# A gated hybrid layer in fp32 on one core: half of the first gate becomes seven block products, MLA's heads follow one another sooner

## The chip, the cores and the metric

The kernel runs on one core of one Trainium2 chip. The core has five engines that run beside each other, each with a queue of its own that it works off in order: PE (TensorE: matmuls and transposes; its weight loads, PEld, overlap them), DVE (VectorE), ACT (ScalarE), POOL (GpSimd) and SP (SyncE, which here only issues DMAs). The metric is the device time of one execution in microseconds, as a median of several.

## What is computed

One layer of a decoder on 512 tokens with 2048 features, in float32, batch 1. Cut to what matters here:

```python
xn = rmsnorm(h, g_mix)
(q_a, k_c, ..., c_q, c_kv, k_r, gate_a, gate_b) = split(xn @ w_in)     # gate_a, gate_b: 2048 columns each
o_a = nsa_attention(...)                    # 16 heads
o_b = mla_attention(c_q, c_kv, k_r, ...)    # 16 heads
mixed = sigmoid(gate_a) * (o_a @ w_o_nsa) + sigmoid(gate_b) * (o_b @ w_o_mla)
h = h + mixed @ w_out
h = h + memory_cross_attention(rmsnorm(h), rmsnorm(mem), ...)   # 256 memory tokens, 4 heads of 128
h = h + square(relu(rmsnorm(h) @ w_ff1)) @ w_ff2
return rmsnorm(h, g_final)
```

The two gates are plain products of the normalised input, 512 x 2048 by 2048 x 2048 each. A sigmoid is made as (1 + tanh(half)) / 2.

## The kernel before

**A product in three matmuls.** Every operand is split into a high and a low part in PE's fp32r format: ACT casts the high part (L444, L447, L1534, L1616), DVE subtracts it to get the low one (L445, L448, L1539, L1621). A product is hi x hi + hi x lo + lo x hi, three matmuls (L437 to L439; in the block products L1765 to L1767).

**Two ways to make a large product.** *Plain chunk* (`chunk`, L546): 512 output columns, all 16 k tiles, four row tiles of 128 tokens; the weights come as a stream of units of 512 KB through `Stream`, loaded by SP into two raw buffers and split a few units ahead. *Block products* (`Mlp` and its kin): two by two blocks in rows and in the contraction, with sums of blocks in place of some products, so that seven products do the work of eight. For weights, the sums are made by the DMA itself, which adds what it reads to what lies there (`accum_op`, L1529); for x, DVE adds blocks (L1589 to L1595). `Gates` (L1954) makes the second gate so: 2 column groups of 1024, seven products each, `NP` = 14.

**Main work and side work.** Python writes each engine's instructions in one fixed order. `Side` (L348) holds attention as a queue of steps, each a few instructions for PE, DVE and ACT: an item of MLA (one head) has 5 steps of scores and 6 of values of the head before, 11 in all; NSA has two items per head. After each k tile of the main work, `side.run(rate)` writes `rate` steps, and one step of the *post*, which prepares what the last chunk left in the four row buffers R: rotary embedding (`rope`, L513, four instructions on POOL per row tile) and the turning of the heads to features (`heads_T`, L530: four transposes on PE, one for each row tile, then a split). A post that isn't through by the last k of the next chunk is written out there without main work between (`end_post`); `ft` doesn't do so. If `heads_T` finds no free slot of the 40 in SBUF, it waits for later steps to free one. An attention group of four heads yields empty steps until its four q and four k heads are turned (`mla_attend`, L1208).

**MLA's stage** (`mla`, L1213). `gate(c)` is a plain chunk of the first gate with Tanh at the end (L1152) and a store of each row tile to `d_g` by a DMA that POOL issues (L1153). `mla_q(q)` makes four heads' q (4 k tiles of 384 columns; post: four ropes, then four heads turned), `mla_kv(q)` their k and v (2 k tiles of 512 columns; post: four heads turned; POOL copies k's rotary part, L1188). The order before:

```
gate 0, q 0, kv 0, [attend 0], q 1, gate 1, kv 1, [attend 1], q 2, gate 2, kv 2, [attend 2],
q 3, gate 3 (feeds), kv 3, [attend 3], [flush]
```

with 4.4 steps per k tile up to kv 0 and 2.6 after it. While gate 3 runs, `fed` gives back the x tiles as they fall out of use and starts `mem_load` (L1266): it loads the memory tokens, and with each call splits one k tile of 128 x 256 (ACT, DVE) and adds its squares (ACT squares, L510; POOL adds, L511). Ten tiles are done in gate 3, six are left for the next stage.

**The memory and second gate's stage** (`mix`, L1237). `mem_k` (L1290) makes the k heads of the memory attention by `ft` (L578): one head is 16 k tiles of three matmuls with 256 columns, and a step of the post comes at every odd k. In head 0, each k also calls `mem_load`. Beside it x is loaded again for the second gate (`x_in`, L1970, SP) and scaled by its gain (`x_gain`, L1977: eight instructions on POOL, L1986, per half of 1024 features and 256 tokens). `mem_v` makes the values, with the first loads and splits of the second gate (`loads`, `ahead`). Then `Gates.run` (L2008): of a group's seven products, every odd half unit splits a weight unit and an x block; all weight loads are issued by POOL (`ONE`). `Mixed` and `Out` follow, with the first gate read back from `d_g`.

`pairs` are five larger buffers: three hold the split c_q and c_kv, two hold v of two attention groups; `mla_kv` takes one and, if none is free, writes side steps until one is.

## Time and profile before

| what | us |
|---|---|
| median of 3 runs | 2788.45 (2785.52 to 2789.39) |
| the profiled execution | 2789.09 |
| its span, first to last instruction | 2787.3 |
| Tanh of the first gate (L1152), first to last start | 605.6 to 861.0 |
| `mem_k`'s first matmul | 867.07 |
| second gate's first product to last Tanh (L2006) | 941 to 1092.2 |

The profile is one execution. Spans are in microseconds from its first instruction, and L437 is line 437 of the kernel. "Idle before" names how long an engine stood still before an instruction and what released it. Matmuls are pipelined: one of 512 columns has a printed length of 0.39 us, but the next starts sooner than that, so prices are read from the distance of starts. The mean granted clock of PE is 0.999.

### The profile page before, as it was taken

What the parts mean: (1) busy time and instruction counts of PE and PEld (TensorE: products, weight loads), DVE (VectorE), ACT (ScalarE), POOL (GpSimd) and SP (SyncE); (2) the same over time, 40 slices, a digit from 0 to 9 for tenths busy, and PEclk for the clock granted to TensorE, in tenths of its full rate; (3) what the DMA queues carried; (4) which work ended last, traced back from release to release, by engine and by line L of the source; (5) the groups of instructions that cost most, each with busy time, mean ns of one, the idle gap of its engine ahead of it and who ended that gap; (6) DMA issues with size and microseconds to landing.
All of it is one profiled execution on the core that took longest, in us unless ns stands there. A gap on an engine that the chain in (4) does not pass through costs nothing.

```text
span 2787.3 us, 37036 instructions
## 1 busy us (share of the span) xinstructions
PE 2765.3 (99%) x13428; PEld 2325.0 (83%) x13428; DVE 2034.2 (73%) x3217; ACT 1592.3 (57%) x2670; POOL 530.9 (19%) x796
## 2 busy tenths in 40 slices
PE   9999999999999999999999999999999999999998
PEld 8888889988888888888888888888888788888887
DVE  6347776766557886878866877777777788888888
ACT  5345556655557675556555766666666444444445
POOL 4021011011116232222200112111211121111111
PEclk9999999999999999999999999999999999999999
DMA  5331112222235798989814899888889998888986
GB/s 180 99 90 62 59 59 67 69 73 80 92 109 177 188 235 202 223 225 255 214 46 135 197 224 219 203 206 218 196 220 254 247 216 220 215 218 220 240 236 156
DMA packets 153383, 476.89 MB, mean 171 GB/s; under 512 B 15728, under 2 KB 40432, under 8 KB 153200
## 3 DMA queue, kind: packets, MB, share of 16 engines
q0 software_dynamic: 63616, 230.72, 39.8%
q1 hardware_dynamic: 71744, 226.25, 23.4%
q10 hardware_dynamic: 17840, 17.57, 1.9%
q8 instruction: 105, 1.72, 0.2%
q14 instruction: 78, 0.64, 0.1%
HBM read 443.01 MB, written 31.46 MB: 170 GB/s over the span
## 4 chain that ended last, share of the span: by engine, by line
PE 92%; DVE 3%; DMA 2%; ACT 2%; issue 1%; POOL 0%; DVEq 0%; ACTq 0%; POOLq 0%
PE mm L1767 10%; PE mm L1766 10%; PE mm L1765 10%; PE mm L437 9%; PE mm L439 8%; PE mm L438 8%; PE st L1767 7%; PE st L1765 7%; PE st L1766 7%; PE st L675 2%; PE o L1765 1%; PE o L1766 1%; PE o L1767 1%; PE st L438 1%; PE st L439 1%
## 5 line engine op out<-in xcount | busy, mean ns | idle before, releaser
L1765 PE MATMUL mm<-s,s 128*128 128x512 f32 x1392 | 545.4, 392 | 0.0
L1767 PE MATMUL mm<-s,s 128*128 128x512 f32 x1392 | 542.4, 390 | 1.1 <-DVE s L1621 1.0
L1766 PE MATMUL mm<-s,s 128*128 128x512 f32 x1392 | 541.8, 389 | 0.0
L1534 ACT CAST s<-d 128x1024 fp32r<-128x1024 f32 x272 | 282.3, 1050 | 245.7 <-DMA d<-wts 224.7
L437 PE MATMUL mm<-s,s 128*128 128x512 f32 (+5 forms) x1012 | 400.5, 396 | 0.0
L1539 DVE TENSOR_TENSOR s<-d,s 128x1024 fp32r<-128x1024 f32 x272 | 329.5, 1220 | 94.2 <-ACT s L1534 93.6
L1539 DVE TENSOR_TENSOR s<-s,s 128x1024 fp32r<-128x1024 f32 x252 | 304.9, 1221 | 105.4 <-ACT s L1534 103.3
L439 PE MATMUL mm<-s,s 128*128 128x512 f32 (+5 forms) x1012 | 381.6, 377 | 0.0
L438 PE MATMUL mm<-s,s 128*128 128x512 f32 (+5 forms) x1012 | 381.1, 377 | 0.0
L1534 ACT CAST s<-s 128x1024 fp32r<-128x1024 f32 x252 | 260.2, 1050 | 182.3 <-DMA s<-wts 161.5
L1765 PE MATMUL st<-s,s 128*128 128x512 f32 x920 | 360.6, 392 | 0.0
L1767 PE MATMUL st<-s,s 128*128 128x512 f32 x920 | 358.3, 389 | 0.0
L1766 PE MATMUL st<-s,s 128*128 128x512 f32 x920 | 358.1, 389 | 0.0
L1767 PEld LDWEIGHTS mm<-s,s 128*128 128x128 f32 x1392 | 261.3, 188 | 56.9 <-DVE s L1621 2.4
L1766 PEld LDWEIGHTS mm<-s,s 128*128 128x128 f32 x1392 | 261.4, 188 | 53.3
L1765 PEld LDWEIGHTS mm<-s,s 128*128 128x128 f32 x1392 | 261.4, 188 | 53.2 <-ACT s L1616 0.3
L1529 POOL DMA_DIRECT2D d<-wts x169 | 149.4, 885 | 813.1 <-DVE s L1539 662.3
L445 DVE TENSOR_TENSOR s<-s,s 128x512 fp32r<-128x512 f32 (+4 forms) x301 | 207.7, 700 | 94.9 <-ACT s L444 93.5
L444 ACT CAST s<-st 128x512 fp32r<-128x512 f32 (+4 forms) x249 | 112.3, 460 | 186.7 <-PE st L675 118.1
L439 PEld LDWEIGHTS mm<-s,s 128*128 128x128 f32 x1012 | 190.0, 188 | 32.6
L444 ACT CAST s<-s 128x512 fp32r<-128x512 f32 (+4 forms) x301 | 177.1, 603 | 59.6 <-PE mm L439 30.4
L437 PEld LDWEIGHTS mm<-s,s 128*128 128x128 f32 x1012 | 191.1, 189 | 20.9
(415 smaller groups left out, 4846.7 us busy)
## 6 DMA issues: line engine op xcount, KB each, us to landing
s<-wts SPq DMA_DIRECT2D x203, 512.0 KB, 3.7
d<-wts POOLq DMA_DIRECT2D x203, 512.0 KB, 8.2
s<-wts POOLq DMA_DIRECT2D x156, 512.0 KB, 8.2
d<-wts SPq DMA_DIRECT2D x69, 512.0 KB, 7.7
PP<-wts POOLq DMA_DIRECT2D x65, 512.0 KB, 8.5
d_u<-s ACTq DMA_DIRECT2D x64, 256.0 KB, 5.0
PP<-wts SPq DMA_DIRECT2D x27, 512.0 KB, 6.5
s<-d_u SPq DMA_DIRECT2D x16, 512.0 KB, 11.8
```

The source lines that it names most:

```text
L437: t.matmul(ps, a.hr, b.hr, start=first, stop=False)
L438: t.matmul(ps, a.hr, b.lr, start=False, stop=False)
L439: t.matmul(ps, a.lr, b.hr, start=False, stop=last)
L444: nc.scalar.copy(o.hr, src)
L445: nc.vector.tensor_sub(o.lr, src, o.hi)
L675: nc.tensor.transpose(ps[:rows, i * 128:i * 128 + 128], p, self.ident)
L1529: self.nc.gpsimd.dma_start(t, src, accum_op=OP.add)
L1534: self.nc.scalar.copy(t.hr, self.raw[i])
L1539: self.nc.vector.tensor_sub(t.lr, r, t.hi)
L1765: m(ps, a.hr, b.hr, start=first, stop=False, skip_group_check=True)
L1766: m(ps, a.hr, b.lr, start=False, stop=False, skip_group_check=True)
L1767: m(ps, a.lr, b.hr, start=False, stop=last, skip_group_check=True)
```

## The change

Columns 1024 to 2047 of the first gate are no longer two plain chunks. They become a third column group of `Gates`, ahead of the two of the second gate: seven more block products, whose result is stored to `d_g` by SP. The loads of the first of all these products are issued by SP and no longer by POOL. MLA's order becomes:

```
gate 0, kv 0, q 0, [attend 0], kv 1, q 1, [attend 1], gate 1 (feeds), kv 2, q 2, [attend 2],
mem_k heads 0 and 1, kv 3, q 3, [attend 3], [flush], mem_k heads 2 and 3, mem_v, second gate
```

with 4.4 steps per k tile up to q 1 and in group 3, and 4.0 in gate 1 and group 2; 1.25 (0.8 before) per two k of `mem_k`, 2.3 (1.8 before) per k tile of `mem_v`. To make room for two groups' heads, the last four x tiles are given back before kv 1; in gate 1 they are loaded again (k = 3) and split again (k = 7 to 10). `mem_load` begins at k = 6 of gate 1 and does eight tiles there (k = 8 to 15), so eight are left for head 0 of `mem_k`. `x_in` and `x_gain` move: the first block's `x_gain` stands ahead of `mem_k` head 2, and the block (1, 1) moves to `mem_v`.

```diff
-T = dict(pace=0.75, r0=4.0, r1=4.4, rm=2.6, rf=4.4, rk=0.8, rv=1.8, rg=1.4)
+T = dict(pace=0.75, r0=4.0, r1=4.4, rm=4.0, rf=4.4, rk=1.25, rv=2.3, rg=1.4)
...
-    for c in range(4):
+    for c in range(2):
         for i in range(8):
             u["ga", c, i] = pack(w[2 * i:2 * i + 2, :, O_GA + 512 * c:O_GA + 512 * c + 512])
-    gb = np.ascontiguousarray(w[:, :, O_GB:O_GB + D]).reshape(2, 4, 2, 128, 2, 2, 512)
-    for c in range(2):
+    gb = np.ascontiguousarray(w[:, :, O_GA + D // 2:O_GB + D]).reshape(2, 4, 2, 128, 3, 2, 512)
+    for c in range(3):
...
     def mla(self, rate):
+        last = range(KT - 4, KT)
         def fed(k):
             if k:
                 self.put(self.X[k - 1])
             if k == 3:
+                self.xagain = [self.slots.get() for _ in range(2)]
+                self.xraw = {i: self.xagain[i % 2][:, 512 * (i // 2 % 2):512 * (i // 2 % 2) + 512] for i in last}
+                for i in last:
+                    self.nc.sync.dma_start(self.xraw[i], self.a["xT"][i])
+            if 6 < k < 11:
+                i = k + KT - 11
+                self.X[i] = self.slot_hl()
+                self.split(self.X[i], self.xraw[i], self.gains[:, G_MIX + i:G_MIX + i + 1])
+            if k == 11:
+                self.put(*self.xagain)
+            if k == 6:
                 self.ml = self.mem_load()
-            if k == 3 or k > 5:
+            if k == 6 or k > 7:
                 next(self.ml)
         self.gate(0, T["rf"])
+        ks, vs = self.mla_kv(0, T["rf"])
         qs = self.mla_q(0, T["rf"])
-        ks, vs = self.mla_kv(0, T["rf"])
-        for q in range(3):
+        self.side.add(self.mla_attend(0, qs, ks, vs))
+        self.put(*(self.X[i] for i in last))
+        ks, vs = self.mla_kv(1, T["rf"])
+        qs = self.mla_q(1, T["rf"])
+        self.side.add(self.mla_attend(1, qs, ks, vs))
+        self.gate(1, rate, fed)
+        self.put(self.X[-1])
+        for q in range(2, 4):
+            r = T["rf"] if q == 3 else rate
+            ks, vs = self.mla_kv(q, r)
+            qs = self.mla_q(q, r)
             self.side.add(self.mla_attend(q, qs, ks, vs))
-            qs = self.mla_q(q + 1, rate)
-            self.gate(1 + q, rate, fed if q == 2 else None)
             if q == 2:
-                self.put(self.X[-1])
-            ks, vs = self.mla_kv(q + 1, rate)
-        self.side.add(self.mla_attend(3, qs, ks, vs))
+                g = Gates(self)
+                self.mem_k(T["rk"], range(2), g)
         self.side.add(self.flush())
...
     def mix(self, g):
...
-        self.mem_k(T["rk"], g)
+        self.mem_k(T["rk"], range(2, 4), g)
...
     def mem_k(self, rate, hs, g):
...
-        for h in range(4):
-            if h < 3:
-                g.x_in(*((0, 0), (1, 0), (1, 1))[h])
-            if h:
-                g.x_gain(*((0, 0), (1, 0), (1, 1))[h - 1])
+        for h in hs:
+            if 0 < h < 3:
+                g.x_in(h - 1, 0)
+            if h > 1:
+                g.x_gain(h - 2, 0)
             ps = self.ft("mk", h, self.MX, rate, n=256, on_k=(on0, on1, None, None)[h])
...
     def mem_v(self, rate, g):
...
+            if u == 0:
+                g.x_in(1, 1)
+            if u == 1:
+                g.x_gain(1, 1)
...
+            self.put(self.mslots[u])
...
 # Mlp.load
-            (self.nc.gpsimd if self.ONE else self.nc.sync).dma_start(t, src)
+            (self.nc.gpsimd if self.one(p) else self.nc.sync).dma_start(t, src)
...
 class Gates(Mlp):
-    CH = 2
+    CH = 3
...
+    def one(self, p):
+        return p
...
     def use(self, p, ps):
...
         c, n = divmod(p, 7)
+        c -= 1
...
             nc.scalar.activation(o, ps[t] if n == 6 else o, AF.Tanh, scale=k.rxh[:, r:r + 1])
+            if c < 0:
+                nc.sync.dma_start(k.d_g[r, :, 1024 + 512 * b:1536 + 512 * b], o)
+                if n > 4:
+                    k.put(C.pop((r, c)))
...
             if n == 0:
-                X = [k.new_st() if p else k.new_mm() for _ in range(2)]
+                X = [k.new_st(), k.new_o() if p > 7 else k.new_st()] if p else [k.new_mm() for _ in range(2)]
```

More of the change, by code (lines that the diff above doesn't have):

```diff
@@ L1218, in fed, with mix @@
             if k == 3:
+                self.xagain = [self.slots.get() for _ in range(2)]
[9 more added lines that the diff above has]
+            if k == 6:
                 self.ml = self.mem_load()
-            if k == 3 or k > 5:
+            if k == 6 or k > 7:
                 next(self.ml)
         self.gate(0, T["rf"])
+        ks, vs = self.mla_kv(0, T["rf"])
         qs = self.mla_q(0, T["rf"])
-        ks, vs = self.mla_kv(0, T["rf"])
-        for q in range(3):
+        self.side.add(self.mla_attend(0, qs, ks, vs))
[9 more added lines that the diff above has]
+            qs = self.mla_q(q, r)
             self.side.add(self.mla_attend(q, qs, ks, vs))
-            qs = self.mla_q(q + 1, rate)
-            self.gate(1 + q, rate, fed if q == 2 else None)
             if q == 2:
-                self.put(self.X[-1])
-            ks, vs = self.mla_kv(q + 1, rate)
-        self.side.add(self.mla_attend(3, qs, ks, vs))
+                g = Gates(self)
+                self.mem_k(T["rk"], range(2), g)
         self.side.add(self.flush())
-    def mix(self):
-        g = Gates(self)
+        return g
+    def mix(self, g):
         m = Mixed(self, g.C)
@@ L1288, in mem_load, with mem_k @@
         self.put(*sl[:2])
-    def mem_k(self, rate, g):
+    def mem_k(self, rate, hs, g):
         nc = self.nc
-        self.kf, self.vf, self.rbm = self.slots.get(), self.slots.get(), self.slots.get()
+        if 0 in hs:
+            self.kf, self.vf, self.rbm = self.slots.get(), self.slots.get(), self.slots.get()
         rbm = self.rbm[:, :256]
@@ L1308, in mem_k @@
         last = None
-        for h in range(4):
-            if h < 3:
-                g.x_in(*((0, 0), (1, 0), (1, 1))[h])
-            if h:
-                g.x_gain(*((0, 0), (1, 0), (1, 1))[h - 1])
+        for h in hs:
[3 more added lines that the diff above has]
+                g.x_gain(h - 2, 0)
             ps = self.ft("mk", h, self.MX, rate, n=256, on_k=(on0, on1, None, None)[h])
-            if h:
+            if last is not None:
                 evac(h - 1, last)
             last = ps
-        evac(3, last)
+        evac(h, last)
     def mem_v(self, rate, g):
@@ L1336, in mem_v @@
                     self.W.mid()
+            self.put(self.mslots[u])
         for i in range(2):
             nc.scalar.activation(self.vf[:, i * 512:i * 512 + 512], ps[i], AF.Copy, scale=self.rm[:, i:i + 1])
-        self.put(self.rbm, self.macc_slot, *self.mslots)
+        self.put(self.rbm, self.macc_slot)
     def to_features(self, d, ps):
@@ L1489, in in_last @@
         return p >= 2 * self.NP - 7
+    def one(self, p):
+        return self.ONE
     def begin(self, k):
@@ L1682, in run @@
             self.W.log += [(n, t, h) for n in ("wo", "w2") for t in range(KT) for h in range(2)]
-            self.W.log += [("gs", c, h, b, i) for c in range(2) for h in range(2) for b in range(2) for i in range(4)]
+            self.W.log += [("gs", c, h, b, i) for c in range(3) for h in range(2) for b in range(2) for i in range(4)]
         self.C, self.out = {}, out
@@ L1968, in in_last, with one @@
         return False
+    def one(self, p):
+        return p
     def x_in(self, t, h):
@@ L2301, in _emit @@
     L.side.pace = 1.0
-    L.mla(T["rm"])
-    out = L.mix()
+    out = L.mix(L.mla(T["rm"]))
     L.cross(1.0, out.run()).run(a["out"])
```

## The prediction, made before the change was run

> **What bounds the kernel now.** The page's busy line and the chain that ended last are read first.
>
> ```profile
> PE 2765.3 (99%) x13428; PEld 2325.0 (83%) x13428; DVE 2034.2 (73%) x3217; ACT 1592.3 (57%) x2670; POOL 530.9 (19%) x796
> PE 92%; DVE 3%; DMA 2%; ACT 2%; issue 1%; POOL 0%; DVEq 0%; ACTq 0%; POOLq 0%
> ```
>
> TensorE (PE) works all the time and carries the chain. Only two things can move the time: how many matmuls there are, and how long PE stands still. So the next view is the table of windows: NSA's tail, MLA's stage, the chunk that feeds the memory tokens, the start of the memory stage, and the whole of the second gate's stage.
>
> ```profile
> 576.00:596.00 20.00, 20.00 (x110) 16.89 (x109) 13.72 (x45) 10.09 (x29) 0.57 (x1) 1.00 0.17 54
> 680.00:700.00 20.00, 20.00 (x105) 16.79 (x104) 11.16 (x32) 8.11 (x21) 0.57 (x1) 1.00 0.21 73
> 840.00:860.00 20.00, 20.00 (x104) 16.89 (x103) 14.81 (x38) 12.81 (x34) 5.76 (x7) 1.00 0.33 118
> 867.00:880.00 13.00, 11.00 (x86) 10.16 (x85) 12.43 (x23) 12.44 (x31) 8.91 (x10) 1.00 0.48 163
> 941.00:1093.00 152.00, 150.93 (x663) 123.84 (x662) 117.56 (x107) 102.35 (x120) 42.28 (x57) 1.00 0.86 209
> ```
>
> The columns are window, length, then busy us of PE, weight load, DVE, ACT and POOL, granted clock, DMA share and GB/s. PE is full in MLA's stage with DVE and ACT half idle; it loses 2.0 us where the memory stage starts (13.00 less 11.00), with DVE and ACT nearly full; and it loses 1.1 us in the second gate's 152 us.
>
> **The matmuls.** The price of one is the distance between starts, not the printed length, for matmuls overlap. The timeline of PE has a plain run in a chunk, first and last of 12, and one in the block products, first and last of 20.
>
> ```profile
> 864.35 0.39 PE L437 MATMUL mm<-s,d 128*128 128x512 f32 x1
> ...
> 866.85 0.39 PE L439 MATMUL mm<-s,d 128*128 128x512 f32 x1
> 1029.67 0.39 PE L1766 MATMUL mm<-s,s 128*128 128x512 f32 x1
> ...
> 1033.98 0.39 PE L1767 MATMUL mm<-s,s 128*128 128x512 f32 x1
> ```
>
> 2.50 / 11 and 4.31 / 19 are both 0.227 us. By the loops, a chunk of the first gate is 16 k tiles x 4 row tiles x 3 = 192 matmuls, so two chunks are 384; a block product is 4 x 2 x 2 x 3 = 48, so seven are 336. That is 48 fewer: 48 x 0.227 = **-10.9 us**. The weights cost DVE and ACT more than before (28 units that are summed by DMA against 16), but the second gate's stage already runs such products with 117.56 us of DVE and 102.35 us of ACT in 152, so seven more go on at PE's pace. The eight stores to `d_g` from there go on SP, which before carries in these products only inputs, and wait for Tanh; no load of weights stands behind them, since from product 1 on those are POOL's. Nothing of this is on the path.
>
> **MLA's heads packed closer.** The same attention steps (11 per head) are laid beside two chunks less. PE's timeline has two groups' last heads turned, POOL's stores of NSA's head pairs give the density there, and the groups by line the price of a split on DVE.
>
> ```profile
> 715.76 1.04 PE L538 MATMUL st<-cst,s 128*96 128x128 f32 x8
> ...
> 795.05 1.04 PE L538 MATMUL st<-cst,s 128*96 128x128 f32 x8
> L753 POOL DMA_DIRECT2D d_nsa<-s x8: 553/568/747, 258.8 to 657.0; - x8
> L445 DVE TENSOR_TENSOR s<-s,s 128x512 fp32r<-128x512 f32 x219 | 157.8, 730 | 53.2 <-ACT s L444 52.0
> ```
>
> A group of four heads takes 795.05 - 715.76 = 79.3 us. Its gate chunk is 192 x 0.227 = 43.6, q and kv are 8.3 and 5.4, eight heads turned some 3.5; 18.5 us are left for 44 steps, 0.42 each. Inside the gate chunk, at 2.6 steps per k tile of 2.7 us, a head takes 11 / 2.6 x 2.7 + 11 x 0.42 = 16.1 us; at 4.0 it takes 12.1, or 1.1 us per step. In NSA an item of 12 steps (two per head, 398.2 / 14) leaves every 28.4 / 2 = 14.2 us, 1.2 us per step, and PE is at 20.00 of 20 us there. But the one chunk left, gate 1, also takes what `fed` does (the window 840:860, DVE 14.81) and four more splits of x. If all of DVE's work grew with the density, it would come to 14.81 / 20 x 16.1 / 12.1 = 99%; only the steps grow, but the splits are new. Bounds: 0, as in NSA, and the four splits wholly on the path, at L445's 0.73 us each, 3 us. I take **+0.8**, near the first, since NSA's row is the nearest in density.
>
> **The start of the memory stage.** This is where the sum is decided. Before, the chunk ahead of `mem_k` is kv 3, whose post only turns heads. After, it is q 2, whose post is four ropes on POOL and then the heads. In `ft` a post step comes at every odd k: ropes at k = 1, 3, 5, 7, the first head's transposes at k = 9, and they read all four row tiles. `mem_load` is now behind: it begins at k = 6 of the chunk, so eight of its 16 tiles (six before) fall into k = 0 to 7 of the first `mem_k`, and each gives POOL an addition (L511). POOL takes its work in order: add, add, rope, four times over. Now the prices.
>
> ```profile
> 867.07 0.28 PE L437 MATMUL mm<-s,s 128*128 128x256 f32 x1
> 867.43 0.28 PE L437 MATMUL mm<-s,s 128*128 128x256 f32 x1
> 867.79 0.60 PE L538 MATMUL st<-cst,s 128*96 128x128 f32 x4
> 870.20 3.69 POOL L511 TENSOR_TENSOR s<-s 128x256 f32<-128x256 f32 x4 [3.73 <-ACT s L510]
> 874.46 1.89 POOL L511 TENSOR_TENSOR s<-s 128x256 f32<-128x256 f32 x2 [0.58 <-ACT s L510]
> 719.39 0.46 POOL L522 TENSOR_TENSOR rp<-s,cst 128x128 f32<-128x128 f32 x1 [10.98 <-ACT s L1162]
> 721.03 0.46 POOL L522 TENSOR_TENSOR rp<-s,cst 128x128 f32<-128x128 f32 x1
> 727.26 0.46 POOL L525 TENSOR_TENSOR s<-rp,rp 128x128 f32<-128x128 f32 x1
> ```
>
> The first addition starts 870.20 - 867.07 = 3.1 us after the stage's first matmul, behind ACT's queue. Six additions take 5.58 us, 0.93 each; eight take 7.4. Four ropes take 727.72 - 719.39 = 8.3 us, of which the first alone, 1.64. So the last rope ends 3.1 + 7.4 + 8.3 = 18.8 us after the start; with ropes at the first one's price (DVE runs dry in the wait) and additions at 0.8, 3.1 + 6.4 + 6.6 = 16.1. PE is at the first head after ten k of 0.36 us and two or three steps of 0.42: 3.6 + 1.1 = 4.7 us. It then waits 11.4 to 14.1 us. Attention can't fill this: group 2's steps yield empty until its eight heads are there, and group 1 is through. I take **+12.0**, and the 2.0 us lost there now are gone: **-2.0**. Below, were the additions all ahead of the ropes and the ropes in cover, nothing beyond those 2.0 us would be lost.
>
> **The clock after so long a wait.** The profile's start and its longest wait are the rows for it.
>
> ```profile
> 0.88 4.21 PE L765 MATMUL st<-sm 128*128 128x128 f32 x18 [0.88 <-POOL mx L762]
> 2178.64 0.39 PE L1767 MATMUL st<-s,s 128*128 128x512 f32 x1
> 2181.22 0.50 PE L1765 MATMUL o<-s,s 128*128 128x512 f32 x1 [2.19 <-ACT s L1839]
> 2182.25 0.40 PE L1766 MATMUL st<-s,s 128*128 128x512 f32 x1
> ```
>
> The first 18 matmuls of 128 columns take 4.21 us, 0.234 each; the eight at 715.76, shown above, 1.04 / 8 = 0.13: about half speed at the start, 4.21 - 18 x 0.13 = 1.9 us lost. After the 2.2 us wait at 2178 the next starts are 0.26 us apart at most, so a short wait costs no clock. Between 0 and 1.9 us I take **+1.5**, nearer the start's row, for 12 us is longer than 2.2. [...]
>
> **Three smaller places.** First, q 3 is followed by k heads 2 and 3. Their POOL queue holds `x_gain` of the first block ahead of the ropes.
>
> ```profile
> 894.52 8.21 POOL L1986 TENSOR_SCALAR d<-d,gains 128x256 f32<-128x256 f32 x8 [0.68 <-DMA d<-xT]
> 718.72 2.16 ACT L1162 ACTIVATE s<-mm,rq 128x384 f32<-128x384 f32 x4 [0.34 <-PE mm L439]
> ```
>
> Eight take 8.21 us. Its input is loaded one `mem_k` head earlier and nothing is queued ahead of it, so it can run under q 3 (48 matmuls of 0.17 us and 13 steps, about 14 us). Then only the ropes count: first evacuation to first rope is 719.39 - 718.72 = 0.7 us, q's last evacuation ends at +0.9, so the ropes end near +7.5, where PE comes at 3.6 + 6 x 0.42 = 6.1: **+1.5** (0 to 3). Second, kv 3 needs a pair that group 1 gives back 12 steps after group 2 begins, and ten lie between: one or two bare steps, **+0.5** (0 to 1.5). Third, the gates' start:
>
> ```profile
> 944.42 0.88 POOL L1529 DMA_DIRECT2D s<-wts  x1 [0.47 <-DMA s<-wts]
> 955.39 0.50 PE L1767 MATMUL mm<-s,s 128*128 128x512 f32 x1 [0.71 <-DVE s L1621]
> 961.37 0.50 PE L1767 MATMUL mm<-s,s 128*128 128x512 f32 x1 [0.26 <-DVE s L1621]
> ```
>
> PE waits 1.0 us for splits that are late because POOL's loads are. The first product's loads move to SP and earlier, which ends that; but the last eight or so attention steps now fall there, on a full DVE. Between -1.0 and +1.5 I take **-0.3**.
>
> Sum: -10.9 + 0.8 + 12.0 - 2.0 + 1.5 + 1.5 + 0.5 - 0.3 = **+3.1 us**. The profiled execution took 2789.09 us and has a span of 2787.3, so 2792.2 by it; on the median of 2788.45, 0.6 us lower, **2791.5 us**. A measurement of this kernel can tell some 0.2%, 5.6 us, from no change.
>
> **The rivals.** *The heads are turned in time.* If POOL gets through its queue by the time PE comes, or the slot supply puts the heads later, into k head 1, the place costs what it costs now, and no clock is lost. For: POOL is busy 19% of the span, and in MLA's stage ropes never hold PE up. Against: there a whole chunk follows a q, here ten short k tiles. Time: 2788.45 - 10.9 + 0.8 + 1.5 + 0.5 - 0.3 = 2780.0. Chance 0.23.
>
> *`x_gain` runs behind q 3's evacuation.* If its DMA lands late, or POOL hangs on a store of `d_mla` in q 3, then the 8.2 us stand ahead of the ropes after all, which end at 0.9 + 8.2 + 8.3 = 17.4 us and not 7.5; PE waits 11.4 us rather than 1.5. It decides when `x_gain` starts later than some 8 us before q 3's end. For: the queue's order, and the 0.68 us that it waited for its DMA before. Against: some 18 us from its issue to q 3's evacuation, and an odd head's store due only after q 3 by the count of steps. Time: 2791.5 + 9.9 = 2801.4. Chance 0.14.
>
> That the change doesn't do what it says can't be: the loops fix the count of matmuls.
>
> **How the numbers follow.** The forecast, a gain given back in one wait, has 0.63, with a range of its own from 2786 (wait 10.5 us, no loss of clock, the small ones at their low ends) to 2797 (14 us, 1.9, high ends of two). The 80% range reaches down to the first rival, 2779.5, and up to 2799, short of the second. Faster by over 0.2% (under 2782.9): the first rival and a little of the forecast's low side, 0.24. Slower (over 2794.0): the second and the forecast's upper side, 0.20. Within: 0.56.
>
> **What would show it.** Right: 48 fewer matmuls on L437 to L439 and L1765 to L1767 together; in the first `mem_k` one wait of PE at L538 of over 10 us, released by POOL L525, with L511 and L522 taking turns on POOL before it; POOL's L1986 inside q 3. Wrong: no wait of over 4 us at L538, or L1986 between q 3's evacuation and its ropes, or waits of PE on DVE all through gate 1.

## The result and the profile after

| what | before | after |
|---|---|---|
| median (fastest to slowest) | 2788.92 us (2785.52 to 2791.96) | 2805.70 us (2804.11 to 2807.91) |
| ratio after / before | | 1.0061, 95% interval 1.0044 to 1.0078 |
| the profiled execution, its span | 2789.09, 2787.3 | 2806.25, 2804.5 |

The change makes the kernel 0.6% slower, 16.8 us by the medians. The prediction said 2791.5 with a range of 2779.5 to 2799.0: the kernel is 6.7 us above its upper end.

The busy line and the chain that ended last, of the profile after:

```profile
PE 2762.2 (98%) x13380; PEld 2321.8 (83%) x13380; DVE 2068.6 (74%) x3237; ACT 1623.3 (58%) x2690; POOL 542.0 (19%) x812
PE 84%; DVE 5%; issue 4%; DMA 4%; ACT 2%; POOL 2%; ACTq 0%; POOLq 0%; DVEq 0%
```

There are 48 matmuls fewer (13428 less 13380), as the loops say. But PE's share of the chain falls from 92% to 84%, and issue, DVE, DMA and POOL take what it lost: PE now stands still for several engines, in several places.

To see how much in each place, take PE's timeline and subtract from the distance between two starts what a matmul costs in a free run (0.227 us for 512 columns, 0.172 for 384, 0.117 for 256, 0.11 for a transpose). What is left is loss: waits and slow clock alike. Summed by stage, in us:

| stretch | before | after | more |
|---|---|---|---|
| start to 600 us | 20.9 | 20.4 | -0.5 |
| 600 us to the first `mem_k` matmul (gates 0 and 1, MLA) | 8.5 | 10.0 | +1.5 |
| `mem_k` head 0 | 2.8 | 15.5 | **+12.7** |
| from there to the first gate product | 1.7 | 8.9 | **+7.2** |
| the first two gate products | 1.1 | 7.6 | **+6.5** |
| the other gate products | 1.0 | 0.2 | -0.8 |
| all that follows | 12.4 | 13.8 | +1.4 |

The sum is +28.0; less 48 x 0.227 = 10.9, it is +17.1, and the spans differ by 17.2. The last row need not be the change's: a second profile of the kernel before, below, has 14.2 there. (The first gate product of the kernel before starts at 937.61, not at 941 as the table ahead of the prediction has it.)

**`mem_k` head 0.** First the windows, of the kernel before and of the one after (columns as in the prediction: window, length, busy us of PE, weight load, DVE, ACT and POOL, granted clock, DMA share, GB/s).

```profile
867.07:878.90 11.83, 9.83 (x75) 9.02 (x74) 11.29 (x20) 11.28 (x29) 7.81 (x9) 1.00 0.53 179
```

```profile
747.00:770.88 23.88, 12.60 (x72) 11.03 (x71) 10.60 (x17) 12.34 (x28) 13.33 (x24) 0.71 0.22 72
750.00:764.00 14.00, 2.71 (x12) 1.41 (x11) 6.07 (x10) 6.20 (x15) 13.07 (x24) 0.70 0.27 94
764.00:768.00 4.00, 4.00 (x20) 3.95 (x20) 1.70 (x3) 1.68 (x3) 0.00 (x0) 0.50 0.00 0
```

The same head takes 23.88 us, where it took 11.83; these windows, here and below, run on through the first k tile of head 1, some 0.4 us. In the second row POOL is busy for 13.07 of 14 us and PE for 2.71. In the third row PE works all the time and waits for nothing, but its clock is 0.50: 4 us for some 2 us of work. Then PE's timeline of that wait, and POOL's (first and last of its run).

```profile
754.05 0.32 PE L538 MATMUL st<-cst,s 128*96 128x128 f32 x1 [2.54 <-POOL s L525]
757.27 0.45 PE L538 MATMUL st<-cst,s 128*96 128x128 f32 x1 [2.91 <-POOL s L525]
760.77 0.45 PE L538 MATMUL st<-cst,s 128*96 128x128 f32 x1 [3.05 <-POOL s L525]
763.75 0.45 PE L538 MATMUL st<-cst,s 128*96 128x128 f32 x1 [2.53 <-POOL s L525]
```

```profile
749.74 1.80 POOL L511 TENSOR_TENSOR s<-s 128x256 f32<-128x256 f32 x2 [12.84 <-ACT s L510]
751.50 0.63 POOL L522 TENSOR_TENSOR rp<-s,cst 128x128 f32<-128x128 f32 x1
...
753.96 1.52 POOL L511 TENSOR_TENSOR s<-s 128x256 f32<-128x256 f32 x2
755.43 0.46 POOL L522 TENSOR_TENSOR rp<-s,cst 128x128 f32<-128x128 f32 x1
...
763.24 0.45 POOL L525 TENSOR_TENSOR s<-rp,rp 128x128 f32<-128x128 f32 x1
```

POOL works off add, add, rope, four times over, from 749.74 to 763.69, and each of the four transposes of the first head is released by the end of one rope. The distances of starts, less a transpose, give 2.70 + 3.12 + 3.39 + 2.87 = 12.1 us.

**Behind q 3.** POOL's timeline and PE's:

```profile
786.42 7.92 POOL L2017 TENSOR_SCALAR s<-s,gains 128x256 f32<-128x256 f32 x8
...
809.58 0.46 POOL L525 TENSOR_TENSOR s<-rp,rp 128x128 f32<-128x128 f32 x1
811.45 0.61 POOL L753 DMA_DIRECT2D d_mla<-s  x1 [1.42 <-ACT PP L598]
812.08 0.48 POOL L522 TENSOR_TENSOR rp<-s,cst 128x128 f32<-128x128 f32 x1
```

```profile
814.25 0.31 PE L538 MATMUL st<-cst,s 128*96 128x128 f32 x1 [1.61 <-POOL s L525]
815.87 0.31 PE L538 MATMUL st<-cst,s 128*96 128x128 f32 x1 [1.31 <-POOL s L525]
```

`x_gain` (L2017) runs from 786.42 to 794.34, from the end of kv 3 into q 3 (whose matmuls run from 789.58), so it is not in the way of the ropes, the first of which starts at 805.87. But between the second rope and the third POOL stands for the store of a head pair (L753): 1.42 us of waiting and 0.61 of issue. PE's two waits come to 1.78 + 1.51 = 3.3 us by starts. That the store costs 1.8 us of them is read from POOL's order; no run takes the store alone out.

**The gates' start.** PE's timeline, then ACT's, DVE's and POOL's:

```profile
871.93 0.71 PE L675 MATMUL st<-cst,PP 128*128 128x128 f32 x5
878.05 0.48 PE L698 MATMUL o<-s,d 128*128 128x128 f32 x1 [5.42 <-DVE s L751]
...
879.08 0.63 PE L1794 MATMUL mm<-s,s 128*128 128x512 f32 x1
879.50 0.63 PE L1795 MATMUL mm<-s,s 128*128 128x512 f32 x1
```

```profile
874.26 1.04 ACT L1562 CAST s<-d 128x1024 fp32r<-128x1024 f32 x1 [1.87 <-DMA d<-wts]
875.59 1.04 ACT L1644 CAST s<-s 128x1024 fp32r<-128x1024 f32 x1 [0.28 <-DVE s L1617]
876.54 0.26 ACT L444 CAST s<-st 128x128 fp32r<-128x128 f32 x1
876.70 0.58 ACT L750 COPY s<-o 64x512 f32<-64x512 f32 x1
```

```profile
877.31 0.69 DVE L751 TENSOR_TENSOR s<-o,s 64x512 f32<-64x512 f32 x1 [0.18 <-ACT s L750]
```

```profile
868.70 0.89 POOL L1557 DMA_DIRECT2D d<-wts  x1 [4.03 <-DVE s L445]
```

The last attention steps now stand among the gate's first products. PE needs the split of the attention weights (cast at ACT L444, 876.54) and the output buffer that the head before leaves (copied at ACT L750, added up at DVE L751, which ends at 878.00 and releases PE). Both instructions of ACT are queued behind two splits of the gate's operands; the first of them, L1562, waits 1.87 us for a weight load that POOL could only issue at 868.70, since it waits 4.03 us for DVE. PE loses 5.6 us, and its next matmuls start 0.42 us apart and not 0.227.

**The clock.** That is the half clock again. The trace's clock records show it in four places after, ahead of the span's end: 632.6 to 636.0, 755.5 to 769.1, 816.9 to 820.3 and 875.0 to 881.8; before, at the span's end alone. The second shows in the windows above; of the last two, the windows after:

```profile
817.00:820.00 3.00, 3.00 (x16) 2.97 (x15) 2.41 (x7) 1.97 (x5) 3.00 (x4) 0.50 0.03 7
875.00:882.00 7.00, 3.95 (x13) 3.26 (x14) 4.69 (x7) 3.68 (x7) 1.58 (x2) 0.52 1.03 193
```

Matmuls of 512 columns start 0.42 us apart there and not 0.227, so work that runs at half clock loses about half of the time it takes: 1.7, 2.65, 1.7 and 1.9 us in the four places, 8.0 together.

The first of the four belongs to this one execution. Seven of the versions below have the same code up to there and the same waits, and none of their profiles shows a half clock near 630 us; the one behind q 3 stands in all five versions that leave q 3 and its queue as they are. So 6.3 us of the 8.0 come back from execution to execution.

### The profile page after: what moved, and what is told of

It reads as the page before. It is cut to its first block, busy times and chain, and to the rows that moved or that the text cites. A ratio compares the mean times of both kernels' runs of the same rounds, so it can differ in the third digit from the quotient of the medians.

```text
span 2804.5 us, 37025 instructions
## 1 busy us (share of the span) xinstructions
PE 2762.2 (98%) x13380; PEld 2321.8 (83%) x13380; DVE 2068.6 (74%) x3237; ACT 1623.3 (58%) x2690; POOL 542.0 (19%) x812
## 4 chain that ended last, share of the span: by engine, by line
PE 84%; DVE 5%; issue 4%; DMA 4%; ACT 2%; POOL 2%; ACTq 0%; POOLq 0%; DVEq 0%
PE mm L1793 10%; PE mm L1794 10%; PE mm L1795 10%; PE mm L437 7%; PE mm L439 7%; PE mm L438 7%; PE st L1793 6%; PE st L1794 6%; PE st L1795 6%; PE st L675 2%; PE o L1793 1%; PE o L1794 1%; PE o L1795 1%; DVE s L1567 1%; DMA d<-wts 1%
## 5 line engine op out<-in xcount | busy, mean ns | idle before, releaser
L1793 PE MATMUL mm<-s,s 128*128 128x512 f32 x1440 | 564.7, 392 | 0.0
L1795 PE MATMUL mm<-s,s 128*128 128x512 f32 x1440 | 561.4, 390 | 0.6 <-DVE s L1649 0.6
L1794 PE MATMUL mm<-s,s 128*128 128x512 f32 x1440 | 560.9, 390 | 0.0
L1562 ACT CAST s<-d 128x1024 fp32r<-128x1024 f32 x293 | 303.8, 1049 | 256.2 <-DMA d<-wts 236.7
L1567 DVE TENSOR_TENSOR s<-d,s 128x1024 fp32r<-128x1024 f32 x293 | 354.4, 1220 | 109.3 <-ACT s L1562 106.0
L1793 PE MATMUL st<-s,s 128*128 128x512 f32 x952 | 373.1, 392 | 0.0
L1562 ACT CAST s<-s 128x1024 fp32r<-128x1024 f32 x257 | 265.1, 1050 | 186.3 <-DMA s<-wts 169.8
L1795 PE MATMUL st<-s,s 128*128 128x512 f32 x952 | 370.8, 389 | 0.0
L1794 PE MATMUL st<-s,s 128*128 128x512 f32 x952 | 370.7, 389 | 0.0
L437 PE MATMUL mm<-s,s 128*128 128x512 f32 (+5 forms) x884 | 349.8, 396 | 0.0
L439 PE MATMUL mm<-s,s 128*128 128x512 f32 (+5 forms) x884 | 332.7, 376 | 0.4 <-DVE s L448 0.4
L438 PE MATMUL mm<-s,s 128*128 128x512 f32 (+5 forms) x884 | 332.3, 376 | 0.3 <-DVE s L448 0.3
L1557 POOL DMA_DIRECT2D d<-wts x184 | 162.9, 885 | 835.5 <-DVE s L1567 648.8
L1795 PEld LDWEIGHTS mm<-s,s 128*128 128x128 f32 x1440 | 270.6, 188 | 57.7 <-DVE s L1649 0.9
L1794 PEld LDWEIGHTS mm<-s,s 128*128 128x128 f32 x1440 | 270.7, 188 | 55.0
L1793 PEld LDWEIGHTS mm<-s,s 128*128 128x128 f32 x1440 | 270.7, 188 | 54.9
L445 DVE TENSOR_TENSOR s<-s,s 128x512 fp32r<-128x512 f32 (+4 forms) x269 | 188.1, 709 | 83.2 <-ACT s L444 81.7
L1795 PEld LDWEIGHTS st<-s,s 128*128 128x128 f32 x952 | 178.7, 188 | 37.4
L1794 PEld LDWEIGHTS st<-s,s 128*128 128x128 f32 x952 | 178.8, 188 | 36.5 <-DVE s L1567 0.2
L1793 PEld LDWEIGHTS st<-s,s 128*128 128x128 f32 x952 | 178.7, 188 | 36.5
L444 ACT CAST s<-st 128x512 fp32r<-128x512 f32 (+4 forms) x249 | 112.4, 461 | 158.8 <-PE st L675 91.0
```

Source lines behind the costliest of these rows:

```text
L437: t.matmul(ps, a.hr, b.hr, start=first, stop=False)
L438: t.matmul(ps, a.hr, b.lr, start=False, stop=False)
L439: t.matmul(ps, a.lr, b.hr, start=False, stop=last)
L444: nc.scalar.copy(o.hr, src)
L445: nc.vector.tensor_sub(o.lr, src, o.hi)
L1557: self.nc.gpsimd.dma_start(t, src, accum_op=OP.add)
```

## The experiments

The theory after the result: the loss is POOL's queue behind q 2 and q 3, ACT's queue at the gates' start, and the half clock behind each of the waits. The rivals: that the waits stand for something else (weights, DVE's density), or that the clock is of no weight. Every ratio is against the kernel before on the same chip; the times of the versions are medians.

**q 2's ropes ahead of the additions.**

```diff
         def post():
             for tt in range(4):
-                self.rope(self.Rv(tt, 384).rearrange("p (n d) -> p n d", n=4), 4, DV, ROT_B, C_CB, C_SB, tt,
-                          nc.vector if q == 0 and tt % 2 else None)
+                if q != 2:
+                    turn(tt)
                 yield
...
         self.chunk("uq", q, 384, evac, rate, nk=4, xs=self.cq, on_k=on_k)
+        if q == 2:
+            for tt in range(4):
+                turn(tt)
```

`turn` holds the rope call as it was.

> The changed kernel with one edit: q 2's four ropes are written as soon as its chunk ends, ahead of the eight additions of mem_load in POOL's queue; its heads are turned at the same k as before. Theory (POOL's order holds the heads): the ropes end some 7.5 us after the first mem_k matmul, PE comes at 4.7, so the waits at L538 in mem_k head 0 fall from 12.1 us to about 3, with less loss of clock behind them (about 1 us less); total about 2805.7 - 9 - 1 = 2796 us. Rival (the heads wait for slots or for the empty attention steps, not for POOL): the waits stay near 12 us and the total near 2805.7.

Measured 2801.37 us, 1.0049 (1.0034 to 1.0064), 5 us worse than expected. The waits for ropes are all but gone: 2.5 us of the 12.1 are left. But the additions are late instead, and ACT's timeline shows who minds:

```profile
753.43 0.42 ACT L510 ACTIVATE s<-s 128x256 f32<-128x256 f32 x1 [4.09 <-POOL s L511]
753.75 0.49 ACT L447 ACTIVATE s<-s,gains 128x256 fp32r<-128x256 f32 x1
```

The buffer of squares has two halves, so ACT's third square waits 4.09 us for POOL's addition, and behind it in ACT's queue stands the split (L447) of the next memory tile, which PE needs. The head takes 17.4 us, and is again at half clock from 753.1 to 760.0. So POOL's order is the cause of the wait, but turning it round moves part of it (0.74 and 0.47 us of standing still at L437 and L438) to its other customer.

**Idle matmuls in q 2's waits.** They overwrite part of q 2's first head and take away nothing that is waited for.

```diff
             for tt in range(4):
+                if fill is not None and v == 0:
+                    for _ in range(10):
+                        self.nc.tensor.matmul(ps, fill[:, :128], fill, start=True, stop=True)
                 self.nc.tensor.transpose(...)
```

> The changed kernel with forty extra matmuls of 512 columns (0.227 us each, 9.1 us together) that nobody reads, ten ahead of each of the four transposes of q 2's first head in mem_k head 0, where PE stands still 2.5 to 3.1 us each time. Theory (PE's clock falls to half because it stands still): PE still waits for the same ropes, but the clock stays at 1.00 over this stretch, so the work after it is not slowed: the 2.7 us lost between 763.9 and 769.1 come back, total about 2803 us, in spite of 9 us more of work. Rival (the half clock has another cause, or extra matmuls just add): clock still 0.50 after the wait, total 2805.7 or up to 2815.

Measured 2803.44, 1.0054 (1.0038 to 1.0071). The window of that head, in this version:

```profile
745.54:767.08 21.54, 19.10 (x111) 15.48 (x111) 10.57 (x17) 12.36 (x28) 13.45 (x24) 1.00 0.20 62
```

POOL's 13.45 us are the same and so is the delay; the clock is 1.00 where it was 0.71, and the head takes 21.54 us and not 23.88. That is the clock's price in this one place: 2.3 us, close to the 2.65 worked out above. The whole time is 2.3 us less as well, but the two intervals overlap, so the evidence is the window.

**Attention run off sooner** in `mem_v`, so that less of it is left for the gates.

```diff
-T = dict(..., rv=2.3, rg=1.4)
+T = dict(..., rv=3.0, rg=1.4)
```

> The changed kernel with mem_v's side rate 3.0 in place of 2.3, so that attention's last eight or so steps are written in mem_v and not in the first block products. Theory (the 5.4 us wait at 872.6 is the last heads' copy standing in ACT's queue behind a split that waits for a weight's DMA): with no attention step left there the wait goes, some 1.3 us at L1795 remain as in the kernel before, and the loss of clock behind it (1.9 us) goes too; total 2805.7 - 4.3 - 1.9 = about 2799.5 us. Rival (product 1's weights are late whatever stands beside them): PE waits as long at L1793 or L1795 for splits, total within 2 us of 2805.7; or mem_v at this density stalls by as much.

Measured 2798.99, 1.0040 (1.0025 to 1.0055), as the theory said. PE's timeline at the same place of the attention, and the window over the gates' start:

```profile
865.69 0.33 PE L698 MATMUL o<-s,d 128*128 128x128 f32 x1 [0.85 <-DVE s L751]
```

```profile
865.00:885.00 20.00, 19.31 (x90) 16.21 (x91) 15.59 (x16) 9.91 (x13) 6.34 (x8) 1.00 0.81 148
```

The wait is 0.85 us, not 5.42; the clock stays at 1.00. The gate's weights are no sooner here: ACT's split waits even longer for its load, but no step of attention stands behind it.

```profile
876.41 1.05 ACT L1562 CAST s<-d 128x1024 fp32r<-128x1024 f32 x1 [3.42 <-DMA d<-wts]
```

The place was worth 0.0021 x 2788 = 5.9 us by the ratios.

**The first product's loads back on POOL**, as all others are.

```diff
     def one(self, p):
-        return p
+        return True
```

> The changed kernel with the first product's four weight loads issued by POOL again. Theory (SP brings them earlier and they are not what is late): POOL's copies stand behind x_gain of block (1, 1) and a store of d_mla, so the first product's splits come later and the gates' start loses 3 to 8 us more, total 2809 to 2814. Rival (the loads' queue does not matter, for the late ones are product 1's): within 2 us of 2805.7.

Measured 2807.44, 1.0070 (1.0055 to 1.0085): not told from the change itself, as the rival said; the loss expected from POOL's queue did not come. PE still waits at the same step:

```profile
875.71 0.48 PE L698 MATMUL o<-s,d 128*128 128x128 f32 x1 [5.45 <-DVE s L751]
```

So which queue loads the first product doesn't matter; where the last attention steps stand does.

**Idle matmuls and attention sooner, together.** In this version 80 idle matmuls of 256 columns stand in q 2's waits (20 ahead of each transpose) and 28 in q 3's (7 ahead of each); as before, they overwrite part of those heads.

```diff
-T = dict(..., rv=2.3, rg=1.4)
+T = dict(..., rv=3.0, rg=1.4)
...
+                if v == 0:
+                    for _ in range(fill):
+                        x = self.MX[0].hr
+                        self.nc.tensor.matmul(ps[:, :256], x[:, :128], x, start=True, stop=True)
```

> The version with attention run off sooner (2799.0), and in the waits of q 2's and q 3's first head idle matmuls of 256 columns (80 and 28; they overwrite part of that head, so its values are not the layer's). They take as long as the waits and remove nothing of what is waited for. Theory (part of the loss is half a clock after the waits): no half clock in 740 to 830, and 4 us less, 2795. Rival (the clock costs nothing that matters, the waits alone do): 2798 to 2800.

Measured 2795.35, 1.0028 (1.0019 to 1.0037), 3.6 us under the version with attention sooner alone (3.3 by the ratios, whose intervals overlap), where 4 were expected. No half clock is left before the span's end. Windows of q 2's wait and of q 3's:

```profile
745.56:767.11 21.55, 19.39 (x151) 18.07 (x151) 10.58 (x17) 12.35 (x28) 13.47 (x24) 1.00 0.19 63
800.00:820.00 20.00, 20.00 (x153) 19.42 (x154) 14.04 (x37) 13.55 (x33) 15.84 (x25) 1.00 0.44 146
```

With matmuls that compute nothing the kernel is faster than without them, by the medians. The clock is a term of its own.

**Ropes on two engines**: every q's ropes at the chunk's end, odd row tiles on DVE.

```diff
         def post():
             for tt in range(4):
-                self.rope(..., nc.vector if q == 0 and tt % 2 else None)
                 yield
...
+        for tt in range(4):
+            self.rope(..., nc.vector if tt % 2 else None)
```

> The changed kernel with the ropes of every q written at once when its chunk ends, rows 0 and 2 on POOL, rows 1 and 3 on DVE; the heads are turned at the same k as before. Theory (the additions and the ropes share POOL's queue; what is long is their sum): two ropes end some 3.5 us after the first mem_k matmul and eight additions 7 us later, so neither the heads (PE comes at 4.7 us) nor the memory tiles wait long: at most 2 us in mem_k head 0, as in the kernel before, no half clock there (-10.1 and -2.7 us); the 3.3 us behind q 3 and the 1.7 us of clock after it go; q 0's 2.3 us shrink by about 1. Total about 2805.7 - 19 = 2787 us. Rival (DVE, already at 80%, becomes what is late): waits on DVE L448 or L445 of 5 us and more in mem_k head 0, total above 2793.

Measured 2797.96, 1.0031 (1.0019 to 1.0042), 11 us worse than expected. Two thirds of the gain on head 0 came (15.75 us, between the 23.88 of the change and the 11.83 of before). DVE's timeline and PE's show the rest:

```profile
748.97 0.63 DVE L522 TENSOR_TENSOR rbc<-s,cst 128x128 f32<-128x128 f32 x1
...
751.80 1.81 DVE L448 SCALAR_TENSOR_TENSOR s<-s,gains,s 128x256 fp32r<-128x256 f32 x2
```

```profile
752.79 0.58 PE L438 MATMUL mm<-s,s 128*128 128x256 f32 x1 [4.05 <-DVE s L448]
```

Now the ropes hold DVE's splits of the memory tiles (L448), and PE waits 4.05 us for one of those. With attention run off sooner as well (both edits shown above):

> The kernel of e5 and mem_v's side rate 3.0 of e3 together. Theory: the gains add, since they lie in different places: about 2787 - 6.7 = 2780 us, 0.3% faster than the kernel before, for 48 matmuls less (10.9 us) and some 2 us of waits more. Rival (each wait removed gives the next one its place, the attention steps being packed too closely for DVE): 2785 us or more, no faster than before.

Measured 2791.76, 1.0010 (1.0001 to 1.0019), 12 us over what was expected and no faster than before, as the rival said. The two gains add up, but the same 4.05 us at L448 stay, and half clocks are back behind other waits, at 753.8, 805.0 and 2187.4 us.

**q before kv** in groups 2 and 3, so that a q's ropes stand beside kv and not beside `mem_k`.

```diff
-            ks, vs = self.mla_kv(q, r)
             qs = self.mla_q(q, r)
+            ks, vs = self.mla_kv(q, r)
```

> The changed kernel with q and kv of groups 2 and 3 in the order of the kernel before (q first), so that kv's post, which has no ropes, stands ahead of mem_k. Theory (the order kv, q is what put POOL's ropes among the additions): the ropes are waited for in kv's two k tiles instead, about 3 us each for groups 2 and 3; in mem_k head 0 some 2.5 us are left, as in the kernel before. Waits 12.1 + 3.3 become about 8.5, total about 2805.7 - 7 - 1 to 2 of clock = 2797 us. Rival (it is the eight tiles of mem_load left over, not the ropes): mem_k head 0 keeps over 8 us of waits, total near 2805.

Measured 2794.70, 1.0018 (1.0009 to 1.0027), near what was expected. It is the smallest edit that takes back most of the loss, but the waits have only moved: kv has two k tiles, too few to cover four ropes, and PE waits 2.9 us in kv 2 and 4.7 us in kv 3, with half clock behind both. Head 0 isn't as before either: two waits for DVE's splits there, 1.9 us together, are followed by a half clock from 757.8 to 764.7.

**Memory tiles sooner**: six more of them beside kv 2 and q 2, so that POOL has two additions left in `mem_k`.

```diff
+            more = (lambda k: next(self.ml)) if q == 2 else None
-            ks, vs = self.mla_kv(q, r)
-            qs = self.mla_q(q, r)
+            ks, vs = self.mla_kv(q, r, more)
+            qs = self.mla_q(q, r, more)
```

> The changed kernel with one edit: six of the eight memory tiles left over are done beside kv 2 and q 2 (one at each k tile), so that two are left for mem_k head 0; ropes and heads as in the change. Theory (the first mem_k head is too short for what is laid beside it: eight additions and four ropes on POOL): POOL then has two additions and four ropes, 9.4 us after the first mem_k matmul, against PE at 4.7: waits at L538 of about 5 us in place of 12.1, clock loss about 1 us less, total about 2805.7 - 8 = 2798 us. Rival (ACT and DVE, and not POOL, set the pace there, or the tiles stall kv 2 and q 2 by as much): total above 2802.

Measured 2801.17, 1.0050 (1.0037 to 1.0064), 3 us over the expectation. PE's timeline:

```profile
753.21 0.45 PE L538 MATMUL st<-cst,s 128*96 128x128 f32 x1 [3.19 <-POOL s L525]
```

Without six additions the four waits are 3.3 + 1.8 + 1.5 + 1.5 = 8.2 us and not 12.1: the rest is the ropes alone, which begin only behind the last two additions, and 10 us of half clock follow (752.7 to 763.0). The additions were a third of the wait, the ropes two thirds.

**All mends**: memory tiles sooner, attention sooner, ropes written at the chunk's end (POOL and DVE up to q 2; POOL alone for q 3, its heads turned two steps later). The first two edits are those shown above; the third:

```diff
         def post():
-            for tt in range(4):
-                self.rope(..., nc.vector if q == 0 and tt % 2 else None)
+            for tt in range(6 if q == 3 else 4):
                 yield
...
+        for tt in range(4):
+            self.rope(..., nc.vector if q < 3 and tt % 2 else None)
```

> The tiles as in e8, mem_v's side rate 3.0, the ropes of each q written at once (q 0 to 2 on POOL and DVE, q 3 on POOL alone with its heads two steps later). Theory (the 48 matmuls are saved in full, and all that ate them were waits of PE with the clock lost behind them): waits in mem_k head 0 under 1.5 us, none behind q 3, 1.4 at the gates' start; against the kernel before -10.9 + 1.8 (gate 1's density) - 1 (q 0) - 1.5 (head 0) + up to 2 of clock = 2777 to 2781 us, 0.3% to 0.4% faster. Rival (packing costs more than waits, or a new wait comes up elsewhere): 2786 us or more.

Measured 2789.21, 1.0006 (0.9997 to 1.0016): level with the kernel before, and some 10 us over the expectation. Head 0 now takes 10.86 us (11.83 before), and the gates start without a wait. One long wait is left. POOL's timeline, ACT's and PE's:

```profile
808.25 0.61 POOL L753 DMA_DIRECT2D d_mla<-s  x1
808.90 7.57 POOL L2019 TENSOR_SCALAR d<-d,gains 128x256 f32<-128x256 f32 x8
```

```profile
813.32 0.58 ACT L750 COPY s<-o 64x512 f32<-64x512 f32 x1 [5.64 <-DMA d_mla<-s]
```

```profile
815.01 0.39 PE L437 MATMUL st<-s,s 96*128 96x256 f32 x1 [3.59 <-DVE s L445]
```

POOL now works off q 3's ropes ahead of `x_gain`, and the store of a head pair stands in the middle of `x_gain`'s sixteen multiplications. ACT's next copy into the same buffer waits 5.64 us for that store, the splits behind it wait too, and PE loses 3.75 us, with half clock from 816.5 to 819.9.

**The first `x_gain` ahead of q 3**, added to all mends.

```diff
             ks, vs = self.mla_kv(q, r, more)
+            if q == 3:
+                g.x_gain(0, 0)
             qs = self.mla_q(q, r, more)
...
-            if h > 1:
+            if h > 2:
                 g.x_gain(h - 2, 0)
```

> The version with all the mends still had one wait of PE behind q 3, 3.75 us at L437, and half a clock behind it (816.5 to 819.9): the copy ACT L750 waits 5.64 us for the store of a head pair (POOL L753), which stands behind eight multiplications of x_gain that now follow q 3's ropes. Here the first x_gain is written ahead of q 3, while POOL is idle. Theory (a wait costs its length and the clock behind it): 5.5 us less, so 2789.2 - 5.5 = about 2783.7, the first version under the kernel before by what a measurement can tell. Rival (what is left lies behind the gates, in waits for weights at L1858 to L1860 that come with any packing): 2787 to 2789, the wait gone, and the excess after the gates' end as large as before it.

Measured 2784.07, 0.9981 (0.9972 to 0.9990): faster than both kernels, by 3.9 us and 21.6 us against their medians. POOL's timeline and the window of head 0:

```profile
774.11 6.84 POOL L2021 TENSOR_SCALAR s<-s,gains 128x256 f32<-128x256 f32 x7
...
800.82 0.61 POOL L753 DMA_DIRECT2D d_mla<-s  x1
```

```profile
746.59:757.45 10.86, 9.35 (x71) 8.47 (x71) 8.98 (x20) 8.14 (x17) 4.99 (x10) 1.00 0.30 97
```

`x_gain` (the view shows seven of its eight instructions) lies where POOL was idle, the store goes 7 us sooner, and no half clock is left before the span's end. By the loss per stretch, as in the table above:

| stretch | before | after | ropes first | attention sooner | two engines | all mends | `x_gain` first |
|---|---|---|---|---|---|---|---|
| 600 us to `mem_k` | 8.5 | 10.0 | 8.6 | 8.6 | 8.6 | 9.2 | 9.3 |
| `mem_k` head 0 | 2.8 | 15.5 | 9.0 | 14.6 | 7.4 | 2.5 | 2.5 |
| to the first gate product | 1.7 | 8.9 | 8.6 | 10.2 | 7.3 | 11.1 | 5.6 |
| first two gate products | 1.1 | 7.6 | 8.6 | 0.8 | 8.0 | 0.7 | 0.6 |
| all that follows the gates | 12.4 | 13.8 | 16.8 | 12.5 | 14.9 | 18.2 | 14.2 |

Of the 10.9 us, 3.9 are still lost between head 0 and the gates, in single waits of 1 us and less. They are probably the price of attention at its higher density, but nothing was run against those.

**The kernel before once more**, unchanged.

> The kernel before, unchanged, as a control for single profiles. Theory (the half clocks in the memory stage come from the change): no half clock before the span's end, mem_k's first head again with waits of under 1 us each, and the stretch from the second gate's end to the last matmul within 2 us of 1685.9 us. Rival (a profile of the kernel before can show them as well): a half window somewhere, or that stretch longer by 3 us or more.

One execution, 2789.85 us; its stages up to the gates are those of the first profile to 0.1 us in most rows. The 1.0 us of waits for splits at the gates' start, from which the prediction took its lower bound there, is 0.34 here. And it shows one half clock, in the feed-forward part. PE's timeline of this second profile:

```profile
2177.09 0.39 PE L1767 MATMUL st<-s,s 128*128 128x512 f32 x1
2180.34 0.50 PE L1765 MATMUL o<-s,s 128*128 128x512 f32 x1 [2.87 <-ACT s L1839]
...
2182.19 0.63 PE L1767 MATMUL st<-s,s 128*128 128x512 f32 x1
2182.62 0.63 PE L1765 MATMUL st<-s,s 128*128 128x512 f32 x1
```

It is the place from which the prediction read that a short wait costs no clock. There it was 2.2 us; here it is 2.9, and the matmuls after it start 0.43 us apart. So a half clock by itself doesn't speak for the change, and some 2 us of what follows the gates differ between these two executions. The rival was right for the half clock; for the loss that follows the gates, 14.2 us here against 12.4, the theory's 2 us held.

## Why the prediction was wrong, step by step

| step of the sum | predicted | measured |
|---|---|---|
| 48 matmuls fewer | -10.9 | -10.9 |
| density in gate 1, and kv 3's pair | +1.3 | +2.0 |
| heads held up in `mem_k` head 0 | +12.0 | +12.1 |
| the old wait there gone | -2.0 | -2.5 |
| behind q 3 | +1.5 | +3.3 |
| the gates' start | -0.3 | +4.6 |
| the clock | +1.5 | +8.0 |

The measured column comes from the table by stretch: the stretch up to the gates is 7.2 us more, of which 3.3 are the waits behind q 3 and 1.7 the clock, which leaves 2.2 for density there; in gate 1 it is 1.5 less 1.7, -0.2. So the nearness of +1.3 and +2.0 is luck: gate 1, where the prediction put 0.8, costs nothing, and the 2.2 us lie between head 0 and the gates, where it had only the 0.5 for kv 3's pair. The gates' start is 5.6 us of wait less the 1.0 of before. (NSA's density, on which the 0.8 leant, was also misread: its last store, 77.6 us after the one before, stands in the mean, and the others are 52 to 55 us apart. Without it an item leaves every 13.4 us and not 14.2, 1.1 us per step, the density of the change, which speaks for 0 as well.)

*The wait behind q 2, the term that decided the sign, was right in place, releaser and size.* It came as four waits of about 3 us and not one of over 10, since each transpose needs one row tile and so one rope. The experiments bear its working out: without the ropes' place in the queue 2.5 us are left, without six additions 8.2.

*The rival with `x_gain` behind q 3's evacuation was wrong as to this change*: `x_gain` was through at 794.34, ahead of q 3's ropes. Its mechanism is real, though. In the version with all mends, which writes the ropes first, `x_gain` and the store did stand in each other's way.

*The rival with the heads in time was wrong*, and the last changed version shows what it was worth: with the heads in time there, the gates started and the store sent, 2784.07, where the rival had 2780.0.

*The step that failed first is the clock.* The prediction put +1.5 us behind one wait, and took from the row at 2178 us that "a short wait costs no clock". It does at times: waits of 3.3 us in sum behind q 3, broken by one transpose, were followed by a half clock of 3.4 us, as were waits of 2.3 us in sum between q 0 and kv 1; before, the same three waits come to 2.1 us and cost no clock, and in seven other versions they come to 2.3 us and cost none. (The row at 2178 us holds one gap of 0.33 us, from 2181.22 to 2181.55, and not 0.26 at most; the clock was 1.00 there even so. The start's row has matmuls 0.234 us apart, but the trace has no clock record ahead of 9.81 us, so that the clock slowed them isn't shown.) There were four places, 8.0 us, one of which, 1.7 us, is this execution's; behind q 2 alone it was 2.65, where 1.5 stood. Idle matmuls in two of the places gave 3.6 us back.

*The second is the gates' start.* The prediction saw that "the last eight or so attention steps now fall there, on a full DVE", and put -1.0 to +1.5 us. The bound was taken from DVE. What held PE was ACT's queue: a copy for attention, behind a split that waits for a DMA, behind POOL, behind DVE. DVE was full, as the prediction had it (busy for 8.93 of the 9 us from 866 to 875), and stands at the far end of that chain; the way from there through POOL's issue, the load and ACT's order was not in the sum. With attention run off sooner, the place costs 0.85 and the time falls by 5.9 us.

*The third is small*: behind q 3 the prediction counted the ropes alone. The store of a head pair, which it named in a rival as what might hold `x_gain`, held the third rope: 2.0 us of POOL's time, by the trace 1.8 on PE. The ropes themselves, 1.5, were right.

So of the 13.7 us between the 16.8 measured and the 3.1 forecast, 6.5 are the clock (1.7 of them this execution's alone), 4.9 the gates' start and 1.8 the store; the rest are terms of under 1 us.

## What to carry to other kernels

A wait of the bound engine costs its length and may cost the clock behind it: price a new wait of the size of those here (PE stood still for 1.63 to 3.10 us of the 3.41 us before each of the four half clocks of the profile after) with some 1.7 us more, an estimate from the half clocks of 3.4 us above, and several in a row as one. Where two streams of work are packed closer, look for the shared in-order queues (here POOL's additions, ropes, gains and stores, and ACT's copies and splits) and ask of each instruction that can wait what stands behind it; moving work ahead of it in the same queue moves the wait to the next customer. What took waits away here was work put into an engine's idle time, or shared with a second engine. A gain in the count of matmuls is worth having only when those queues are mended with it: of 10.9 us the kernel got 3.9 in the end.

## What the runs showed of the hardware

The clock records of the profile after give PE's half clocks by start and length: 632.61 us for 3.413 us, 755.49 for 13.653, 816.93 for 3.413, 874.95 for 6.827, and one at the span's end, from 2800.07 on. The later starts lie 122.88, 184.32, 242.35 and 2167.46 us behind the first, which are 36, 54, 71 and 635 times 3.4133 us to within 0.02 us; the four lengths are 1, 4, 1 and 2 times as much. Counted from the span's start these five lie 1.14 us past such a multiple, and the one half clock in the first profile of before, at its span's end (2781.43), lies 2.98 us past one.

In the 3.41 us before the first four starts PE stood still, by the printed ends of its matmuls, for 1.63, 3.10, 2.04 and 2.32 us. In the first profile of before, the wait of 2.19 us that ended at 2181.22 was followed by a clock of 1.00; the one of 2.87 us in its second profile, by matmuls 0.43 us apart and not 0.227. So about 2 us of standing still cost the clock in one place and not in another. What decides between them isn't shown.
